# Sixteen of 48 column blocks of a conditioning map, moved from a feed-forward layer to the S5 scans

## The chip, the cores and the metric

One core of one Trainium2 chip runs the whole program in one launch. The metric is the device time of one execution in microseconds, and the lower the better.

## What is computed

The reference is a two-layer trunk for 128 context tokens and 1024 latent tokens of width 1024, in fp32. Every sub-layer is scaled, shifted and gated by a conditioning map of that layer, `w_ada[l]`, which is 1024 × 6144: six vectors of 1024 (shift, scale and gate of the mixer, then of the feed-forward part).

```
for l in range(DEPTH):                                   # DEPTH = 2
    mod = silu(c_in) @ w_ada[l] + b_ada[l]
    sh1, sc1, g1, sh2, sc2, g2 = split(mod, 6)
    h = modulate(rmsnorm(x, norm1_g[l]), sh1, sc1)
    if l % 2 == 0:  m = conv_fourier_mixer(h, ...)       # layer 0
    else:           m, fin = s5_mixer(h, ...)            # layer 1
    x = x + g1 * m
    h = modulate(rmsnorm(x, norm2_g[l]), sh2, sc2)
    x = x + g2 * (silu(h @ w_gate) * (h @ w_up)) @ w_ffn_out[l]
```

`s5_mixer` drives 64 groups of 16 channels through a 64-state complex diagonal recurrence in both directions, then takes GELU and a gated linear unit (GLU).

## The kernel before

**Stages.** Layer 0's mixer, the first feed-forward layer (about 480 to 1300 us), the S5 scans (about 1310 to 1481 us), the GLU, the second feed-forward layer. Big matmuls are three fp32r products each (lines 123 to 125).

**The map of layer 2** (in the code the second of the two layers has the number 1) is made as side work of the first feed-forward layer. The 6144 columns are 48 blocks of 128. For one block, `ada_load` (line 280) brings 512 KB into the tile `araw`, and `ada_rows` (line 299) does eight fp32 matmuls into an `ada` bank (line 304; each is two on the hardware), one copy on ACT into a row tile `arow` (line 306) and a store of the row to `ada1_d` in DRAM. Every few blocks `ada_sums` (line 309) reads the rows back transposed with eight small strided loads (`acol`, line 314), and adds them on POOL into `modt[1]`. `ada_scale` makes the scale vectors from it. The loop at the end of `table_steps` sets the pace: one block at every seventh turn of the tables' side work, the sums of six blocks at a time. All DMAs of this work are issued from ACT's queue. Blocks 32 to 47 are the scale and the gate of the second feed-forward part.

**The scans** run over eight feature tiles f (class `S5`, `run` at line 1243). `front(f)` makes S = E·U on PE (line 1162) and copies it into the pair of tiles D on ACT (line 1168; half of them on VectorE for f = 0). `scan(f)` is twelve operations on VectorE (lines 1184 to 1195) that use the tables T, D and tiles R and V of which there are two each. `back(f)` makes the products Y on PE (M·U at line 1213, fz·state at line 1219), copies them on ACT into y (line 1222), stores y to `yd_d` from ACT's queue (line 1226) and loads it back into `zp`, transposed, from POOL's queue (line 1230). `gelu(f)` on ACT (line 1236) turns zp into a tile of `xall`. `spill(f)` (line 1239) stores a piece of x from POOL's queue. U, E, T, M and fz come in by SP's queue; the scans' input u goes out to `u_d` in DRAM and comes back as U by SP's queue as well. Tiles come from pools with a fixed number of buffers: who asks for a tile whose buffers are all in use waits for the last reader of the oldest.

**The GLU** (`Glu.run`, line 1374) splits the tiles of `xall` into two fp32r halves `zz` on ACT and VectorE (lines 1294, 1295), with the last two `gelu` in between, and starts its products.

The order of the instructions on each engine is laid out by a scheduling layer, not by the text of the code alone.

Of the kernel before, what the change touches and what calls it, by code (L numbers as in the profile page):

```python
# [11 lines left out]
F32 = mybir.dt.float32  # L12
# [8 lines left out]
NF = D // 128  # L21
# [3 lines left out]
CW = 384  # L25
# [31 lines left out]
def kernel(  # L57
# [7 lines left out]
    nc = tc.nc  # L65
    V, S, G, PE = nc.vector, nc.scalar, nc.gpsimd, nc.tensor
    uid = [0]

    def nm(p):
        uid[0] += 1  # L70
        return f"{p}{uid[0]}"
# [24 lines left out]
    ada1_d = dram.tile([128, 48 * 128], F32, name="ada1_d")  # L96
# [199 lines left out]
        PE.matmul(po[:, 0:2], row, sel, start=True, stop=True)  # L296
        V.tensor_scalar(modt[l][:, s, :], po[:, 0:2], vec_a[:, 48 * l + s:48 * l + s + 1], None, op0=OP.add)

    def ada_rows(pool, s, raw):

        ps = aux("ada")
        for k in range(8):
            j = k % 4
            PE.matmul(ps[32 * j:32 * j + 32, :128], cond[:, k, :], raw[:, k, :], start=(k < 4), stop=(k >= 4))  # L304
        row = pool.tile([128, 128], F32, tag="arow", name=nm("arow"), bufs=2)
        S.activation(row, ps[:, :128], AF.Copy)
        nc.scalar.dma_start(ada1_d[:, s * 128:s * 128 + 128], row)

    def ada_sums(pool, b0, nb):

# [523 lines left out]
    def table_steps(P, pool, tb):  # L834
# [156 lines left out]
        raw, ns, summed, turn = ada_load(pool, 1, 0), 0, 0, 0  # L991
        for f in range(8):
            ct = prepare(f, *nxt)
            yield
            for q in range(4):
                if q % 2 == 0:
                    both = []
                if q == 1 and f < 7:
                    nxt = fetch(f + 1)
                for i, _ in enumerate(batch(f, q, ct, both)):  # L1000
                    if ns % 6 == 0 and turn % 7 == 5 and summed < ns:
                        ada_sums(pool, summed, 6)
                        summed = ns
                    if turn % 7 == 0 and ns < 48:
                        ada_rows(pool, ns, raw)
                        ns += 1
                        if ns < 48:
                            raw = ada_load(pool, 1, ns)
                    turn += 1
                    yield  # L1010
# [35 lines left out]
    class S5:  # L1046
# [52 lines left out]
        @staticmethod  # L1099
        def groups(f):  # L1100
            return ((0, 2), (2, 2), (4, 2), (6, 2)) if f in (0, NF - 1) else ((0, 3), (3, 3), (6, 2))

        BUFS = {"U": 4, "T": 2, "T1": 2, "d0": 2, "D": 6, "R": 2, "V": 2, "yz": 3}

# [128 lines left out]
        def gelu(self, f):  # L1233
# [2 lines left out]
            S.activation(zt[:, :LAT].rearrange("p (c t) -> p t c", t=T8), zv[:, :, LX:], AF.Gelu_apprx_tanh)  # L1236
            S.activation(zt[:, LAT:].rearrange("p (c t) -> p t c", t=T8), zv[:, :, :NC_CTX], AF.Gelu_apprx_tanh)

        def spill(self, f):
            cs = slice((NCH - 1) * CW, TOK)  # L1240
            nc.gpsimd.dma_start(x_d[f][:, cs], self.x[f][:, cs])

        def run(self):
            self.front(0)
            for f in range(NF):
                self.scan(f)
                if f + 1 < NF:
                    self.front(f + 1)
                if f + 2 < NF:
                    self.load_e(f + 2)  # L1250
                if f:
                    self.back(f - 1)
                if f + 2 < NF:
                    self.load_in(f + 2)
                if f and f + 1 < NF:
                    self.load_out(f + 1)
                if f + 2 < NF:
                    self.load_t(f + 2)
                    self.decay(f + 2)
                if f > 1:  # L1260
                    with tc.issue_after(self.last.ins):
                        self.gelu(f - 2)
                self.spill(f)
            self.back(NF - 1)

    def states_out(P, fin):
        st = P.t("st")[0:64, :256].rearrange("s (q p r) -> s q p r", q=2, r=2)
        for i in range(2):
            ps = aux("fin")
            PE.transpose(ps[:64, :128], fin[i], ident)  # L1270
            V.tensor_copy(st[:, :, :, i], ps[:64, :128].rearrange("s (q p) -> s q p", q=2))
        nc.sync.dma_start(new_state[0, 0].rearrange("d (k q) p r -> k d q (p r)", q=2),
                          st.rearrange("s q p r -> s q (p r)"))
# [8 lines left out]
    class Glu:  # L1282
# [87 lines left out]
        def run(self, gelu, forms0):  # L1370
            for c in (0, 1):
                for f in range(NF - 2):
                    self.split(f, c)
            for f in (NF - 2, NF - 1):
                with tc.issue_after(self.last.ins):
                    gelu(f)
                for c in (0, 1):
                    self.split(f, c)
            self.weights(0)
            sg = self.products((0, 1), 0)  # L1380
            for f in range(NFK, NF):
                for c in (2, 3):
                    self.split(f, c)
            for c in (0, 1):
                self.load_x(c)
            self.add(sg, 0)
            todo = [(f, c) for f in range(NFK) for c in (2, 3)]
            for i in range(1, NF):
                self.output((0, 1), i)
                for _ in range(2):  # L1390
                    if todo:
                        self.split(*todo.pop(0))
            self.load_x(2)
            self.load_x(3)
            for c in (0, 1):
                self.store_x(c)
            work = None
            for i in range(NF):
                if i == 1:
                    self.norm.finish(0)  # L1400
                    self.norm.finish(1)
                    work = forms0()
                self.output((2, 3), i, work or iter(()))
            for _ in work:
                pass
            for c in (2, 3):
                self.store_x(c)
            for c in (2, 3):
                self.norm.finish(c)
# [342 lines left out]
    with ExitStack() as right:  # L1752
# [4 lines left out]
        with tc.tile_pool(name="act0", bufs=1, reuse_waits="tile") as act, \  # L1757
                tc.tile_pool(name="tmp0", bufs=2, reuse_waits="tile") as tmp0, \
                tc.tile_pool(name="big0", bufs=5, reuse_waits="tile") as big0:
            P = Pools(hp, act, tmp0, 3)  # L1760
# [4 lines left out]
        with tc.tile_pool(name="act1", bufs=1, reuse_waits="tile") as act, \  # L1765
# [5 lines left out]
            def fill():  # L1771
                with tc.tile_pool(name="tb0", bufs=5, reuse_waits="tile") as tb0:
                    yield from tb.build(P, tb0)
                with tc.tile_pool(name="wk", bufs=1, reuse_waits="tile") as wk:
                    g = table_steps(P, wk, tb)
                    yield from g
                    ada_scale(1, 0, G)
                    ada_scale(1, 1, G)

            s5 = {}  # L1780

# [24 lines left out]
        with tc.tile_pool(name="big2", bufs=1, reuse_waits="tile") as big2, \  # L1806
                tc.tile_pool(name="tmp2", bufs=2, reuse_waits="tile") as tmp2:
            P = Pools(None, None, tmp2, 1)
            s5, s5_in = s5["run"], s5["in"]
            s5.begin(P, big2, zq)  # L1810
            for i, _ in enumerate(s5_in.chunk(NCH - 1, s5.load_in)):
                if i == 2:
                    s5.outputs()
            s5.run()
            states_out(P, s5.fin)
    with ExitStack() as right, late as left:
        def pool(name, side, bufs=1):
            st = right if side == "right" else left
# [84 lines left out]
```

## Time and profile before

| | us |
|---|---|
| three executions | 2509.4, 2514.0, 2515.5 |
| median | 2514.0 |
| the profiled execution | 2516.9 |
| its span | 2514.9 |
| PE busy | 2420.1 (96%) |
| DVE busy | 1743.5 (69%) |
| ACT busy | 895.0 (36%) |
| POOL busy | 182.9 (7%) |

The profile is of one execution. A row of a timeline names the start, the time busy, the engine, the line, the operation, output <- inputs, the tile's shape, how often it stands there in a row, and in brackets how long the engine sat idle before it and what released it. "PEclk" is the granted clock of TensorE as a share of its full 2.4 GHz; "DMA share" is the mean busy share of the 16 DMA engines.

### The profile page before, as it was taken

The page shows a single profiled execution, that of the slowest core. Times are in us where ns is not written, and L with a number is a line of the kernel's source. Part 1 is how long each engine was busy: PE and PEld are TensorE (multiplying, and loading weights), DVE is VectorE, ACT ScalarE, POOL GpSimd, SP SyncE. Part 2 cuts the span into 40 slices and gives each one's busy share as a digit, 9 for nine tenths or more (in the row PEclk, how much of TensorE's full clock was granted, in tenths as well). Part 3 has the DMA queues.
Part 4 walks back from the last instruction along what each step waited for, and adds up shares of the span by engine and source line. Part 5 has one row for each costly group of instructions (what it writes and reads, how often), then busy time and mean ns, then how long its engine had stood idle before and what let it go on. Part 6 is the DMA issues. An engine that isn't in the chain of part 4 may idle for free.

```text
span 2514.9 us, 45306 instructions
## 1 busy us (share of the span) xinstructions
PE 2420.1 (96%) x17327; PEld 2344.8 (93%) x17327; DVE 1743.5 (69%) x4619; ACT 895.0 (36%) x1805; POOL 182.9 (7%) x233
## 2 busy tenths in 40 slices
PE   7999999999999999999976899999999999999998
PEld 6999999999999999999976789998999999999998
DVE  7766678988887888887258983658666666645343
ACT  5322443233233333322353552535232232434332
POOL 0000120000000000000020001112000000122110
PEclk9999999999999999999988999999999999999999
DMA  9443342344545455543257973342222212476543
GB/s 261 128 133 94 93 118 62 82 125 120 136 122 134 122 133 132 131 125 82 81 177 261 297 207 106 115 123 85 86 68 70 89 62 88 142 233 206 157 133 103
DMA packets 522680, 328.02 MB, mean 130 GB/s; under 512 B 101000, under 2 KB 492672, under 8 KB 522464
## 3 DMA queue, kind: packets, MB, share of 16 engines
q1 hardware_dynamic: 350432, 236.25, 32.0%
q10 hardware_dynamic: 163680, 58.96, 9.6%
q0 software_dynamic: 8352, 29.92, 3.6%
q8 instruction: 136, 2.23, 0.4%
q14 instruction: 80, 0.66, 0.1%
HBM read 254.04 MB, written 71.01 MB: 129 GB/s over the span
## 4 chain that ended last, share of the span: by engine, by line
PE 81%; DVE 8%; DMA 7%; ACT 2%; issue 1%; ACTq 0%; SPq 0%; POOL 0%; DVEq 0%; POOLq 0%
PE mm L123 19%; PE mm L125 18%; PE mm L124 18%; PE mm L1563 6%; PE mm L1565 6%; PE mm L1564 6%; PE Y L1219 1%; DVE xall L588 1%; DMA yd_d<-y 1%; PE ada L304 1%; DMA zp<-yd_d 1%; DMA hr<-hid_d 1%; DVE tm L831 1%; DMA u_d<-u 1%; PE nst L194 1%
## 5 line engine op out<-in xcount | busy, mean ns | idle before, releaser
L123 PE MATMUL mm<-hh,whi 128*128 128x384 f32 x1392 | 472.5, 339 | 1.1 <-ACT f L448 1.1
L125 PE MATMUL mm<-hh,wlo 128*128 128x384 f32 x1392 | 466.0, 335 | 1.5 <-DVE wlo L117 1.3
L124 PE MATMUL mm<-hl,whi 128*128 128x384 f32 x1392 | 465.8, 335 | 0.0
L117 DVE TENSOR_TENSOR wlo<-wraw,whi 128x1024 fp32r<-128x1024 f32 (+1 forms) x216 | 259.6, 1202 | 227.1 <-ACT whi L116 226.0
L116 ACT ACTIVATE whi<-wraw 128x1024 fp32r<-128x1024 f32 (+1 forms) x218 | 225.7, 1036 | 490.2 <-PE mm L124 363.1
L123 PEld LDWEIGHTS mm<-hh,whi 128*128 128x128 f32 x1392 | 261.5, 188 | 10.9 <-issue 9.0
L125 PEld LDWEIGHTS mm<-hh,wlo 128*128 128x128 f32 x1392 | 261.4, 188 | 4.6 <-issue 2.5
L124 PEld LDWEIGHTS mm<-hl,whi 128*128 128x128 f32 x1392 | 261.6, 188 | 0.2 <-issue 0.2
L588 DVE SCALAR_TENSOR_TENSOR xall<-mm,modt,xall 128x384 f32<-128x384 f32 (+2 forms) x384 | 190.5, 511 | 64.4 <-PE mm L125 63.5
L1563 PE MATMUL mm<-T,wf 128*128 128x288 f32 x640 | 189.6, 296 | 0.0
L1564 PE MATMUL mm<-T,wf 128*128 128x288 f32 x640 | 189.0, 295 | 0.0
L1565 PE MATMUL mm<-T,wf 128*128 128x288 f32 x640 | 188.3, 294 | 0.0
L123 PE MATMUL mm<-hb,whi 128*128 128x384 f32 x528 | 178.6, 338 | 6.9 <-ACT whi L116 6.9
L123 PE MATMUL mm<-hidh,whi 128*128 128x384 f32 x528 | 181.6, 344 | 0.5 <-ACT whi L116 0.5
L125 PE MATMUL mm<-hb,wlo 128*128 128x384 f32 x528 | 178.3, 338 | 1.9 <-DVE wlo L117 1.9
L125 PE MATMUL mm<-hidh,wlo 128*128 128x384 f32 x528 | 177.9, 337 | 0.6 <-DVE wlo L117 0.6
L124 PE MATMUL mm<-hb,whi 128*128 128x384 f32 x528 | 177.7, 337 | 0.0
L124 PE MATMUL mm<-hidl,whi 128*128 128x384 f32 x528 | 177.4, 336 | 0.0
L123 PE MATMUL mm<-zz,whi 128*128 128x288 f32 x512 | 152.4, 298 | 3.1 <-ACT zz L1294 2.1
L124 PE MATMUL mm<-zz,whi 128*128 128x288 f32 x512 | 151.0, 296 | 0.2
L125 PE MATMUL mm<-zz,wlo 128*128 128x288 f32 x512 | 150.9, 296 | 0.0
L185 POOL TENSOR_TENSOR ssq<-ssq,sq 128x384 f32<-128x384 f32 (+1 forms) x75 | 98.4, 1312 | 703.2 <-ACT sq L181 701.0
(388 smaller groups left out, 5454.7 us busy)
## 6 DMA issues: line engine op xcount, KB each, us to landing
wraw<-in_w_ffn_out_dram SPq DMA_DIRECT2D x70, 512.0 KB
wraw<-in_w_ffn_in_dram SPq DMA_DIRECT2D x52, 512.0 KB
araw<-in_w_ada_dram ACTq DMA_DIRECT2D x48, 512.0 KB
wraw<-in_w_glu_dram SPq DMA_DIRECT2D x32, 512.0 KB
araw<-in_w_ada_dram ACTq DMA_DIRECT2D x80, 192.0 KB
wraw<-in_w_out_mix_dram SPq DMA_DIRECT2D x24, 512.0 KB
xall<-in_w_ffn_in_dram SPq DMA_DIRECT2D x20, 512.0 KB
wr<-in_w_ffn_in_dram SPq DMA_DIRECT2D x20, 512.0 KB
```

What stands on the lines that cost most here:

```text
L116: S.activation(hi[:, :n], raw[:, :n], AF.Copy)
L117: eng.tensor_sub(lo[:, :n], raw[:, :n], hi[:, :n].bitcast(F32))
L123: PE.matmul(ps, wh, xs[0], start=start, stop=False)
L124: PE.matmul(ps, wh, xs[1], start=False, stop=False)
L125: PE.matmul(ps, wl, xs[0], start=False, stop=stop)
L185: eng.tensor_add(self.ssq[ch], self.ssq[ch], sq)
L194: PE.matmul(ps[:bw, j:j + 1], part[:, j * bw:(j + 1) * bw], ones, start=part is not sq, stop=part is sq)
L304: PE.matmul(ps[32 * j:32 * j + 32, :128], cond[:, k, :], raw[:, k, :], start=(k < 4), stop=(k >= 4))
L588: V.scalar_tensor_tensor(x[o][:, a:b], ps[:, a - ch * CW:b - ch * CW], gate(l, which, o, s), x[o][:, a:b], op0=OP.mult, op1=OP.add)
L1563: PE.matmul(ps, wh, xh[:, cs], start=kt == 0, stop=False)
L1564: PE.matmul(ps, wh, xl[:, cs], start=False, stop=False)
L1565: PE.matmul(ps, wl, xh[:, cs], start=False, stop=kt == NFK - 1)
```

## The change

The last 16 of the 48 blocks are no longer made in `table_steps` but in a new method `condition(f)` of the scans, two per feature tile, after `spill(f)`. Their loads and the stores of their rows are issued from POOL's queue. `araw` is there a tile with one buffer in the pool `tmp2`; the row is a slice of a tile with the tag "t", three buffers, in the scans' first pool. The pace in `table_steps` goes from a block every 7 turns to one every 11, the sums from 6 blocks to 8. The sums of the 16 blocks and the second scale are made in `Glu.run`, once both x loads are issued, before the first `add`. The final states use a "t" tile of the same pool.

```
-    def ada_rows(pool, s, raw):
+    def ada_rows(row, s, raw, queue):
...
-        row = pool.tile([128, 128], F32, tag="arow", name=nm("arow"), bufs=2)
         S.activation(row, ps[:, :128], AF.Copy)
-        nc.scalar.dma_start(ada1_d[:, s * 128:s * 128 + 128], row)
+        queue.dma_start(ada1_d[:, s * 128:s * 128 + 128], row)
...
-                    if ns % 6 == 0 and turn % 7 == 5 and summed < ns:
-                        ada_sums(pool, summed, 6)
+                    if ns % 8 == 0 and turn % 11 == 8 and summed < ns:
+                        ada_sums(pool, summed, 8)
                         summed = ns
-                    if turn % 7 == 0 and ns < 48:
-                        ada_rows(pool, ns, raw)
+                    if turn % 11 == 0 and ns < S5.ADA:
+                        ada_rows(pool.tile([128, 128], F32, tag="arow", name=nm("arow"), bufs=2), ns, raw, nc.scalar)
                         ns += 1
-                        if ns < 48:
+                        if ns < S5.ADA:
                             raw = ada_load(pool, 1, ns)
...
+        ADA = 32
...
+        def condition(self, f):
+            n = (48 - self.ADA) // NF
+            for s in range(self.ADA + n * f, self.ADA + n * f + n):
+                raw = self.P.tmp.tile([128, 8, 128], F32, tag="araw", name=nm("araw"), bufs=1)
+                nc.gpsimd.dma_start(raw, w_ada[1, :, s * 128:s * 128 + 128].rearrange("(k p) c -> p k c", p=128))
+                row = self.pools[0].tile([128, CW], F32, tag="t", name=nm("arow"), bufs=3)[:, :128]
+                ada_rows(row, s, raw, nc.gpsimd)
...
                 self.spill(f)
+                self.condition(f)
             self.back(NF - 1)
...
             for c in (0, 1):
                 self.load_x(c)
+            ada_sums(self.tmp, S5.ADA, 48 - S5.ADA)
+            ada_scale(1, 1, G)
             self.add(sg, 0)
...
                     ada_scale(1, 0, G)
-                    ada_scale(1, 1, G)
```

How this moves instructions is seen in the order of the built programs. On PE, at the beginning of the scans, behind the last norm (`nrb`), before:

```order
L206 MATMUL nrb_15772<-ident,rq_15740 128x128 x3
L1162 MATMUL S_15844<-U_15781,E_15768 64x145 x4
...
L1162 MATMUL S_15890<-U_15781,E_15770 64x145 x4
L1162 MATMUL S_15930<-U_15790,E_15797 64x145 x6
...
L1162 MATMUL S_15968<-U_15790,E_15799 64x145 x4
L1162 MATMUL S_16016<-U_15982,E_15978 64x145 x6
```

and after:

```order
L206 MATMUL nrb_15498<-ident,rq_15466 128x128 x3
L304 MATMUL ada_15727<-araw_15724,cond 32x128 x8
L304 MATMUL ada_15741<-araw_15738,cond 32x128 x8
L1164 MATMUL S_15570<-U_15507,E_15494 64x145 x4
...
L304 MATMUL ada_15932<-araw_15929,cond 32x128 x5
L1164 MATMUL S_15598<-U_15507,E_15494 64x145 x4
...
L304 MATMUL ada_15932<-araw_15929,cond 32x128 x3
L1164 MATMUL S_15656<-U_15516,E_15523 64x145 x6
...
L304 MATMUL ada_15946<-araw_15943,cond 32x128 x8
L304 MATMUL ada_16138<-araw_16135,cond 32x128 x8
L304 MATMUL ada_16152<-araw_16149,cond 32x128 x8
L304 MATMUL ada_16344<-araw_16341,cond 32x128 x2
L1164 MATMUL S_15770<-U_15708,E_15704 64x145 x6
```

The names with U_15781, U_15790 and U_15982 before (U_15507, U_15516 and U_15708 after) are tiles 0, 1 and 2. Two blocks now stand before S of tile 0, one is split around its second half, and block 3 and those up to the first two matmuls of block 6 stand between S of tile 1 and S of tile 2.

On ACT, where S of tile 1 is copied into its two D tiles, before:

```order
L1168 ACTIVATE D_15928<-S_15962 128x2x145
L1173 ACTIVATE D_15928<-h_15131 128x4
L1168 ACTIVATE D_15929<-S_15938 128x3x145
L1168 ACTIVATE D_15929<-S_15954 128x3x145
L1168 ACTIVATE D_15929<-S_15968 128x2x145
```

and after, where the pair is D_15654 and D_15655:

```order
L1170 ACTIVATE D_15654<-S_15688 128x2x145
L1175 ACTIVATE D_15654<-h_14857 128x4
L305 ACTIVATE arow_15945<-ada_15946 128x128
L1170 ACTIVATE D_15655<-S_15664 128x3x145
L1170 ACTIVATE D_15655<-S_15680 128x3x145
L1170 ACTIVATE D_15655<-S_15694 128x2x145
```

The row of block 3 now stands between the copies of the two tiles. On VectorE those that read tile 1's second D come before the scan of tile 0 (R_15626), here after; before it was the same with other numbers:

```order
L1187 TENSOR_TENSOR V_15753<-T_15529,D_15655 128x1168
L1189 TENSOR_TENSOR D_15655<-T_15527,D_15655 128x1168
L1186 TENSOR_TENSOR R_15626<-T_14851,D_15568 128x584 x2
L1188 TENSOR_TENSOR R_15626<-R_15626,V_15627 128x584
L1190 TENSOR_TENSOR D_15568<-T_14853,D_15568 128x584
```

Nothing moved on VectorE itself. On PE at the end of the scans, where the products Y of tile 6 begin, there were only rows of lines 1213 and 1219 before; after:

```order
L1221 MATMUL Y_16897<-D_16386,fz_16528 128x145
L304 MATMUL ada_16951<-araw_16948,cond 32x128 x8
L1215 MATMUL Y_17005<-U_16523,M_16731 128x145
L1215 MATMUL Y_17006<-U_16523,M_16731 128x145
...
L1221 MATMUL Y_17005<-D_16592,fz_16734 128x145
L304 MATMUL ada_16965<-araw_16962,cond 32x128 x8
```

Between the two blocks stand 15 rows of Y. The same pattern stands at Y of tile 7.

## Rows read from the trace of the kernel before

**Rows 1.** Stretches: us; busy PE, PEld, DVE, ACT, POOL; PEclk, DMA share, GB/s.

```profile
600.00:800.00 200.00, 197.12 (x1439) 188.15 (x1439) 162.66 (x651) 63.53 (x151) 3.83 (x8) 0.99 0.51 129
...
1304.00:1316.00 12.00, 2.15 (x13) 1.69 (x13) 8.19 (x28) 6.60 (x9) 0.54 (x1) 0.59 0.42 123
1316.00:1343.00 27.00, 13.33 (x146) 12.73 (x148) 15.62 (x21) 6.87 (x25) 0.00 (x0) 0.69 1.03 370
...
1402.00:1457.00 55.00, 46.73 (x590) 41.73 (x586) 54.90 (x43) 25.77 (x69) 1.59 (x3) 0.97 0.89 281
1457.00:1481.00 24.00, 23.72 (x298) 20.97 (x294) 22.12 (x33) 8.43 (x14) 1.06 (x2) 1.00 0.66 191
1481.00:1500.00 19.00, 15.96 (x107) 14.48 (x107) 12.49 (x30) 17.88 (x38) 2.33 (x3) 1.00 0.61 183
```

**Rows 2.** Timeline of DVE: tile 1, scan 0, then tiles 4 and 7.

```profile
1331.48 1.38 DVE L1185 TENSOR_TENSOR V<-T,D 128x1168 f32<-128x1168 f32 x1 [4.61 <-ACT D L1173]
1332.89 1.37 DVE L1187 TENSOR_TENSOR D<-T,D 128x1168 f32<-128x1168 f32 x1
1334.86 1.44 DVE L1184 TENSOR_TENSOR R<-T,D 128x584 f32<-128x584 f32 x2 [0.59 <-DMA u_d<-u]
...
1402.87 1.37 DVE L1185 TENSOR_TENSOR V<-T,D 128x1168 f32<-128x1168 f32 x1
...
1457.39 0.77 DVE L1185 TENSOR_TENSOR V<-T,D 128x584 f32<-128x584 f32 x1
```

**Rows 3.** Timeline of PE at the beginning of the scans.

```profile
1317.47 11.21 PE L1162 MATMUL S<-U,E 128*64 128x145 f32 x128 [8.18 <-DMA U<-u_d]
1340.85 5.59 PE L1162 MATMUL S<-U,E 128*64 128x145 f32 x64 [12.16 <-DMA U<-u_d]
```

**Rows 4.** Timeline of PE around one block in the feed-forward layer.

```profile
489.53 0.34 PE L124 MATMUL mm<-hidl,whi 128*128 128x384 f32 x1
489.71 0.34 PE L125 MATMUL mm<-hidh,wlo 128*128 128x384 f32 x1
489.98 0.65 PE L304 MATMUL ada<-araw,cond 128*32 128x128 f32 x16
490.55 0.44 PE L123 MATMUL mm<-hidh,whi 128*128 128x384 f32 x1
490.83 0.34 PE L124 MATMUL mm<-hidl,whi 128*128 128x384 f32 x1
```

**Rows 5.** Line 304: idle time of PE before it (us, times), by releaser.

```profile
  issue: 8.7, 37
```

**Rows 6.** The tile zp: its eight loads (issue in ns), and their landing.

```profile
L1230 POOL DMA_DIRECT2D zp<-yd_d x8: 528/531/539, 1372.6 to 1486.8; - x8
...
DMA to landing us min/median/max: 4.0/5.4/8.2
```

**Rows 7.** The chain that ended last, 1370 to 1500 us: start, us, what.

```profile
1395.20 8.19 DMA zp<-yd_d
1403.47 11.64 DMA yd_d<-y
...
1481.30 4.97 DMA yd_d<-y
1486.82 4.29 DMA zp<-yd_d
```

**Rows 8.** Timeline of POOL: the last store of x before the scans.

```profile
1304.25 0.54 POOL L1241 DMA_DIRECT2D x_d<-xall  x1 [2.76 <-DVE xall L588]
```

**Rows 9.** Timeline of PE: the beginning of Y of tile 6.

```profile
1457.37 0.76 PE L1213 MATMUL Y<-U,M 128*128 128x145 f32 x4
1458.07 0.76 PE L1219 MATMUL Y<-D,fz 64*128 64x145 f32 x8
```

**Rows 10.** Issues of the sums' loads (ns); timeline of ACT at the last gelu.

```profile
L314 ACTq DMA_DIRECT2D acol<-ada_d x64: 366/556/2242, 561.2 to 1146.0; - x64
...
1491.12 2.16 ACT L1236 ACTIVATE xall<-zp 128x1024 f32<-128x1024 f32 x1 [0.96 <-DMA zp<-yd_d]
```

More of the change, by code (lines that the diff above doesn't have):

```diff
@@ L1263, in run, with states_out @@
                 self.spill(f)
+                self.condition(f)
             self.back(NF - 1)
-    def states_out(P, fin):
-        st = P.t("st")[0:64, :256].rearrange("s (q p r) -> s q p r", q=2, r=2)
+    def states_out(pool, fin):
+        st = pool.tile([128, CW], F32, tag="t", name=nm("st"), bufs=3)[0:64, :256].rearrange("s (q p r) -> s q p r", q=2, r=2)
         for i in range(2):
@@ L1814 @@
             s5.run()
-            states_out(P, s5.fin)
+            states_out(s5.pools[0], s5.fin)
     with ExitStack() as right, late as left:
```

## The prediction

> **What bounds the kernel now.** I read the busy times by stretch first, because the change takes work from one stage and puts it into another, and what a microsecond of TensorE is worth differs between the two. From 600 to 800 us, inside the first feed-forward layer, PE is busy 197.1 of 200 us [rows 1]: whatever is taken off PE there comes off the end. In the scan stage (about 1335 to 1457 us) the bound is VectorE: DVE is busy 54.9 of 55 us between 1402 and 1457, PE 46.7 and ACT 25.8 [rows 1]. One feature tile takes (1457.39 − 1402.87) / 3 = 18.17 us of it [rows 2]. So PE has idle time there, but not at its two ends. At the front, 1316 to 1343 us, PE and DVE wait for data: the DMA share is 1.03 at 370 GB/s [rows 1], and PE stood idle 8.18 us before the first S matmuls and 12.16 us before those of tile 2, both times released by U [rows 3]. At the tail, 1457 to 1481, PE is busy 23.72 of 24 us [rows 1]: the Y products of the last two tiles are the critical path.
>
> **The part that is taken out.** Each block is 16 hardware matmuls. At 489.98 us one stands between two ordinary ones: the start before it is 489.71, the start after it 490.55, 0.84 us for what takes 0.18 elsewhere in the same rows (489.53 to 489.71), and the next one starts 0.28 later instead of 0.18 [rows 4]. So a block costs 0.66 + 0.10 = 0.76 us, and 16 cost 12.2. Over all 48 blocks the engine also sat idle 8.7 us under "issue" before them [rows 5], a third of which is 2.9. That bounds the gain by 12.2 and 15.1 us; I take **−14**, nearer the upper end, since the idle time stood in front of these very instructions. The three ways in which the sums are cut differently (blocks of 8, every 11 turns) touch ACT's queue and POOL there, which have time: nothing.
>
> **The front of the scans, the term I am least sure of.** The order of the changed kernel shows what now stands ahead of scan 0. araw has one buffer, so the loads are a chain: load, 16 matmuls, next load. Blocks 0 and 1 stand on PE before S of tile 0, block 2 is split around its second half, and block 3 comes after S of tile 1. On ACT the copy of block 3's row stands ahead of the three copies that make tile 1's second D. And on DVE V and D of tile 1 stand ahead of R of tile 0, that is, ahead of the whole of scan 0. So scan 0 now waits for the fourth load of a serial chain. Its price is four landings. The trace shows no such load at this place. The nearest rows are the zp loads, the same queue and 580 KB instead of 512: 4.0, 5.4 and 8.2 us to landing (least, median, most) [rows 6], 8.19 us in the one of the critical chain where the DMA was full, while the y store of 580 KB took 11.64 [rows 7]. I take about 5.7 for the first two, at 1304 to 1316 where the share is 0.42 [rows 1], and 8.2 for the other two, where it is 1.03. The last spill is issued at 1304.25 and takes 0.54 [rows 8], so block 0 lands at 1310.5; its matmuls cost 0.65 at full clock [rows 4] and about 1.15 here by estimate, since the granted clock of this stretch is 0.59 [rows 1]: 1311.7. Block 1: 1317.5, done 1318.6. Only then S of tile 0 begins, 1.1 us later than the 1317.47 of before [rows 3]. Block 2 lands at 1326.8; the second half of S(0), 2.8 us (11.21 us for 128 matmuls [rows 3], so 2.8 for 32), stands between its first five matmuls and its last three, so it is done, and block 3's load issued, at about 1330.5. Block 3 lands at 1338.7 and is done at 1339.8. Then the row's copy, three copies of some 0.45 (1.6 us together by estimate), V 1.38 and D 1.37 [rows 2]: R of tile 0 starts at about 1344.2 instead of 1334.86 [rows 2], which is **+9**. With landings of 4.0 the chain ends at about 1331, right behind S of tile 1, and nearly all of it is hidden in the 8 and 12 us that PE waited anyway: +1. With 11.6 for the last two it is +17. Three more blocks stand before S of tile 2; by the same landings it ends near 1363, Y of tile 0 near 1375, and scan 2, which needs the R and V buffers that Y of tile 0 frees, would begin at about 1376: just enough, so they add nothing. The loads of U and E that share the queue engines are delayed at most by the added bytes, 4 × 512 KB at 370 GB/s = 5.7 us, a second way to the same few microseconds.
>
> **The middle.** From tile 2 on one or two blocks of 0.65 us [rows 4] fall to each 18.17 us, of which PE has 18.17 − 18.17 × 46.73/55 = 2.7 idle [rows 1]. They hide, but for the last four. Two blocks stand around S of tile 6 and two around S of tile 7, and the Y product of tile 5 ends at 1457.37, when scan 7's first V starts at 1457.39 (it needs the buffer) [rows 2, 9]: no slack at all. Four times 0.65 is 2.6, plus a wait for the second load of a pair: **+3**, between 0 and 6.
>
> **The tail.** The last four blocks stand before and inside Y of tiles 6 and 7, when nothing but PE works toward the end: 4 × 0.6 = 2.4 us for certain. In each pair the second load can start only when the first block's matmuls are done, and only 15 hardware rows of Y (about 2.2 us by estimate: 12 rows of M and fz take 1458.07 − 1457.37 + 0.77 = 1.47 [rows 9]) separate the two. With a landing of 5.4 [rows 6] PE waits 5.4 + 0.1 − 2.2 = 3.3 us twice. Together **+9**, between 6.2 (4.0 us) and 14.6 (8.2 us). What follows the last Y (the store of y, 4.97, its load, 4.29, gelu on ACT) [rows 7] is moved as it is.
>
> **The start of the GLU.** The sums of the 16 blocks are eight small strided loads, issued from ACT's queue. In before such an issue took 0.366, 0.556 and 2.242 us (least, median, most) [rows 10]. Seven stand ahead of the last splits, 7 × 0.56 = 3.9 us, on an engine busy 17.88 of 19 us [rows 1] that waited only 0.96 before the last gelu [rows 10]. Some of it falls beside work that PE already has: **+2**, between 0 and 4. POOL's adds and the scale behind them are needed only in the next norm: nothing.
>
> **Sum.** −14 + 9 + 3 + 9 + 2 = +9. The profiled execution took 2516.9 us, 2.9 above the median of 2514.0, so 2525.9 on its footing is **2523** as a median. 0.3% is 7.5 us, about what a measurement of this kernel can tell from no change; +9 lies just beyond.
>
> **The rivals.**
> *Quick loads.* If a 512 KB load lands in 4.5 to 5 us even in the full stretch, the chain of four ends at about 1332, its delay shrinks to +3 (R at 1332 + 1.6 + 2.75 = 1336.3, and 1.5 for the added bytes), the tail to +7, the middle to +1 and the GLU's start to +1: −14 + 12 = −2, 2512. For it: the median landing of zp is 5.4 with 580 KB [rows 6]. Against it: the one zp that met a full DMA took 8.19 and the store beside it 11.64 [rows 7].
> The Trainium skill's page "DMA: Bandwidth & Descriptors", section "Queues, rings and completion order", says that each DMA engine takes turns between the queues that have work, a packet from each. By that rule a load on POOL's queue gets half of the engines beside SP's queue however long that one is, some 5 us by estimate for 512 KB at half of 370 GB/s with its start, which is this rival's time of 2512. The trace disagrees in the 8.19 us.
> *Everything hides.* With landings of 4.0 us throughout, the whole gain of up to 15.1 remains, less the tail's 6.2, which no landing removes, and 1 at the front: −8, 2506. This needs the least row of the trace everywhere.
> *The transfers become the bound.* 16 × 512 KB = 8.4 MB are added to stretches with a share of 0.89 to 1.03 at 281 to 370 GB/s [rows 1], 23 to 30 us of all engines. The ring of y store (11.64), zp load (8.19) [rows 7] and gelu, one per tile, takes 19.8 us of them against a tile's 18.17 [rows 2]; if each of the six middle tiles is stretched by some 1.5 us of added transfer, that is +9 on top: +18, 2532. It decides once a tile's two loads lengthen the ring by more than its slack. In before the share falls to 0.66 only after 1457 [rows 1].
> *A blocked descriptor writer.* DVE is busy without a gap in the scans, and POOL's loads would have to wait for it. Here the zp issues took 0.53 us while DVE was busy 54.9 of 55 us [rows 6, 1], so nothing is added for it.
> The Trainium skill's page "SBUF — State Buffer", section "A bandwidth-pool intuition that's wrong (but worth ruling out)", gives such a DMA 3.1 us instead of 0.62 beside a DVE copy; 16 of them at 2.5 us more would be 40 us by estimate if all were on the path. The zp rows speak against it.
>
> **How the numbers follow.** My forecast (+9, its own range +3 to +17) has 0.47. Quick loads 0.28, everything hidden 0.12, the transfers 0.11, the blocked writer 0.02. Range: 2508 to 2538, which leaves out the lowest part of the hidden case and the largest sums. Of the forecast all but a little lies above +7.5 or close below it; I count that little with the quick loads: faster by over 0.3% 0.12, within 0.3% 0.30, slower 0.58.
>
> **What would show it.** In the changed profile: the feed-forward layer some 14 us shorter; the first three S groups waiting for araw instead of U; R of tile 0 at about 1330 in its own time (1344 less 14); Y of tile 6 interrupted for some 3 us by a wait for araw; landings of araw between 5 and 9 us. It would be wrong if araw lands in 4 us beside a full DMA, if S of tile 0 starts as early as before, or if the scans' tiles take more than 18.2 us each.

## The result and the profile after

The changed kernel takes 2569.5 us (median of 4), the kernel before on the same chip 2514.6: a ratio of 1.0214, 95% interval 1.0200 to 1.0227, 55 us slower. Slower was forecast, but by 9 us, and 2569.5 lies far outside 2508 to 2538. The profiled execution has a span of 2565.9 us, 51.0 above the 2514.9 of before.

The same stretches as in [rows 1], from the changed kernel (us; busy PE, PEld, DVE, ACT, POOL; granted clock, DMA share, GB/s):

```profile
600.00:800.00 200.00, 195.60 (x1375) 187.66 (x1376) 162.91 (x655) 62.83 (x146) 0.70 (x3) 1.00 0.45 114
800.00:1000.00 200.00, 193.51 (x1360) 184.89 (x1359) 168.39 (x683) 59.63 (x135) 1.87 (x8) 1.00 0.46 112
...
1402.00:1457.00 55.00, 47.58 (x590) 42.19 (x588) 49.45 (x39) 23.45 (x64) 6.49 (x10) 0.91 1.01 338
1457.00:1481.00 24.00, 18.55 (x230) 15.74 (x228) 17.64 (x14) 8.54 (x23) 3.46 (x5) 0.86 0.59 182
1481.00:1500.00 19.00, 12.31 (x128) 10.39 (x126) 18.63 (x24) 3.88 (x8) 3.43 (x5) 0.73 0.68 209
```

The kernel before has for 800 to 1000 us, a row that [rows 1] leaves out:

```profile
800.00:1000.00 200.00, 198.03 (x1446) 187.52 (x1444) 169.94 (x684) 61.26 (x140) 3.08 (x9) 1.00 0.52 127
```

Two things stand there. In the feed-forward layer PE is *less* busy in the same time, 195.6 and 193.5 of 200 us against 197.1 and 198.0 (197.8 and 195.0 in a second profile of the kernel before): the matmuls are gone and idle time has come instead. In the scans VectorE is no longer full (49.45 of 55), PE is idle too, and the granted clock has fallen to 0.73 at the end.

To see where the 51 us arise I read the start of the same instruction in both profiles. Each step is the difference of two neighbouring marks:

| stage, up to | before | after | added here |
|---|---|---|---|
| last norm ahead of the scans (nrb) | 1308.4 | 1306.4 | −2.0 |
| scan 0 begins (R of tile 0) | 1334.9 | 1344.4 | +11.5 |
| scan 2 begins (V of tile 2) | 1366.5 | 1378.2 | +2.2 |
| scan 6 begins (V of tile 6) | 1439.2 | 1456.4 | +5.5 |
| scan 7 begins (V of tile 7) | 1457.4 | 1481.3 | +6.7 |
| last Y done (fin on PE) | 1480.3 | 1525.6 | +21.4 |
| GLU's first product | 1481.7 | 1527.5 | +0.6 |
| second feed-forward layer, first product of T and wf (its weight load) | 1733.7 | 1783.3 | +3.7 |
| end of the span | 2514.9 | 2565.9 | +1.4 |

So the feed-forward layer gave 2 us instead of 14, and the scans took 47. The waits behind it, timeline of VectorE after (against [rows 2]):

```profile
1341.70 1.37 DVE L1187 TENSOR_TENSOR V<-T,D 128x1168 f32<-128x1168 f32 x1 [10.44 <-ACT D L1175]
1344.40 1.44 DVE L1186 TENSOR_TENSOR R<-T,D 128x584 f32<-128x584 f32 x2
...
1378.22 1.38 DVE L1187 TENSOR_TENSOR V<-T,D 128x1168 f32<-128x1168 f32 x1 [2.11 <-PE Y L1221]
...
1456.44 1.38 DVE L1187 TENSOR_TENSOR V<-T,D 128x1168 f32<-128x1168 f32 x1 [5.45 <-DMA T<-t_d]
...
1481.34 1.45 DVE L1187 TENSOR_TENSOR V<-T,D 128x584 f32<-128x584 f32 x2 [6.66 <-PE Y L1221]
```

And on PE, where the blocks' loads had not landed (the groups of line 304, after):

```profile
1307.87 1.08 PE L304 MATMUL ada<-araw,cond 128*32 128x128 f32 x16 [0.60 <-DMA araw<-in_w_ada_dram]
1316.39 1.08 PE L304 MATMUL ada<-araw,cond 128*32 128x128 f32 x16 [7.44 <-DMA araw<-in_w_ada_dram]
...
1338.85 1.08 PE L304 MATMUL ada<-araw,cond 128*32 128x128 f32 x16 [5.50 <-DMA araw<-in_w_ada_dram]
...
1441.47 1.08 PE L304 MATMUL ada<-araw,cond 128*32 128x128 f32 x16 [5.06 <-DMA araw<-in_w_ada_dram]
...
1466.85 1.08 PE L304 MATMUL ada<-araw,cond 128*32 128x128 f32 x16 [5.45 <-DMA araw<-in_w_ada_dram]
...
1492.10 1.08 PE L304 MATMUL ada<-araw,cond 128*32 128x128 f32 x16 [6.69 <-DMA araw<-in_w_ada_dram]
...
1512.63 1.08 PE L304 MATMUL ada<-araw,cond 128*32 128x128 f32 x16 [4.27 <-DMA araw<-in_w_ada_dram]
```

The last four are the second blocks of the pairs at S of tiles 6 and 7 and inside Y of tiles 6 and 7. In the group of line 304 between 1300 and 1530 us PE stood idle 56.7 us for araw (busy, mean ns, idle before):

```profile
L304 PE MATMUL ada<-araw,cond 128*32 128x128 f32 x256 | 15.5, 362 | 56.7 <-DMA araw<-in_w_ada_dram 56.7
```

Each of these waits has a tail of its own. Around the one at 1492 us, PE's rows that [rows 9] shows at 0.76 take 1.33 and 1.34; the granted clock is 0.51 from 1492 to 1499 and 1.00 from 1499 on:

```profile
1493.11 1.33 PE L1221 MATMUL Y<-D,fz 64*128 64x145 f32 x6
1494.37 1.33 PE L1215 MATMUL Y<-U,M 128*128 128x145 f32 x4
1495.63 1.34 PE L1221 MATMUL Y<-D,fz 64*128 64x145 f32 x8
...
1499.37 0.76 PE L1215 MATMUL Y<-U,M 128*128 128x145 f32 x4
```

And the same by stretch (columns as above):

```profile
1492.00:1499.00 7.00, 6.90 (x54) 5.92 (x56) 6.97 (x10) 0.28 (x1) 1.44 (x2) 0.51 0.52 169
1499.00:1505.00 6.00, 6.00 (x80) 5.37 (x76) 2.59 (x5) 0.82 (x2) 0.00 (x0) 1.00 0.02 4
```

That is 6.3 us of Y (1493.11 to 1499.37) for what takes about 3.3 at full clock: a wait of 6.69 us costs some 9.6. Behind the waits of 5.06, 5.45 and 4.27 us the granted clock was 0.50 for 6.0, 4.3 and 6.6 us, which lost 2 to 3 us each.

### The profile page after: what moved, and what is told of

Its sections match the earlier page's. It is cut to its first block, busy times and chain, and to the rows that moved or that the text cites. A ratio compares the mean times of both kernels' runs of the same rounds, so it can differ in the third digit from the quotient of the medians.

```text
span 2565.9 us, 45279 instructions
## 1 busy us (share of the span) xinstructions
PE 2435.5 (95%) x17327; PEld 2355.8 (92%) x17327; DVE 1740.5 (68%) x4619; ACT 896.2 (35%) x1805; POOL 202.3 (8%) x256
```

## Experiments

Chips differ by some us (the kernel before: 2514.6, 2519.9, 2520.5, 2521.7 and 2515.8 us as the median beside each group of runs), so ratios are against the kernel before on the same chip, and stages are compared by the time *between* marks: last norm to last Y (172 us before), and GLU's first product to the first one of T and wf in the second feed-forward layer (252 us before; called the GLU's time below). Each profile is of one execution. In the profiles without blocks in the scans, the kernel before and the relieved ones further down among them, last norm to last Y spreads from 171.9 to 176.1 us, so a few us there tell nothing.

**The feed-forward part alone.** In `run`, the new call is taken out, and the sums read rows 16 to 31 in place of 32 to 47:

```
-                self.condition(f)
...
-            ada_sums(self.tmp, S5.ADA, 48 - S5.ADA)
+            ada_sums(self.tmp, S5.ADA, 48 - S5.ADA, S5.ADA - 16)
```

> The 16 blocks are left out altogether (32 are made in the feed-forward layer, the sums at the GLU's start read other rows). My theory: the feed-forward layer gives back only what the profile after shows, the last norm 2.0 us earlier than before, because VectorE's table work is next in line there; the scans are as before; the GLU starts 5 us later for the sums' loads on ACT. So about 2517, within 0.3% of before. Rival: the 14 us are really saved and something in the scans takes them back; then 2514 - 14 + 5 = 2505.

Measured 1.0043 (1.0025 to 1.0062), 11 us slower than before, though 16 blocks less are made. Neither expectation held. The GLU took 255.8 us instead of 252, as in the changed kernel, but the feed-forward layer gave nothing that the profile shows: the last norm stands at 1313.7 us. (The profiled execution, 2524.0 us, was the fastest of the five.)

**The same with the sums' loads on SP's queue** (`queue.dma_start` with `nc.sync` in `ada_sums`).

> As the run without the 16 blocks, but the eight loads of the sums are issued from SP's queue. Theory: the issues on ACT stood between the last splits and cost 5 us there, so this is 4 to 5 us faster than the run without the blocks, about 2512. Rival: the GLU's start is late for the scans' tail alone; then no difference between the two.

Measured 1.0042 (1.0026 to 1.0058): no difference to the run before, but not for the rival's reason. The sums are dear wherever they are issued. SP takes 14.78 us to issue the eight loads. POOL's adds of the sums, which here stand ahead of POOL's x loads (in the run before, behind the first two), begin only at 1500.61, and the x loads follow at 1502.17. VectorE's first add to x waits 8.62 us for them, the low halves of the weights (`wlo`) stand behind that add, and PE waits 8.21 us for `wlo`; the GLU takes 261.7 us. The timeline of SP, POOL, VectorE and PE:

```profile
1482.58 14.78 SPq L315 DMA_DIRECT2D acol<-ada_d  x8
1510.36 1.50 SPq L113 DMA_DIRECT2D wraw<-in_w_glu_dram  x2
...
1500.61 0.32 POOL L316 TENSOR_TENSOR acol<-acol 128x64 f32<-128x64 f32 x1 [12.09 <-ACT whi L116]
...
1502.17 1.87 POOL L1311 DMA_DIRECT2D xall<-x_d  x2
...
1508.73 0.46 DVE L1352 TENSOR_TENSOR xall<-xall,sg 128x288 f32<-128x288 f32 x1 [8.62 <-DMA xall<-x_d]
1509.11 2.35 DVE L117 TENSOR_TENSOR wlo<-wraw,whi 128x1024 fp32r<-128x1024 f32 x2
...
1510.38 0.61 PE L125 MATMUL mm<-zz,wlo 128*128 128x288 f32 x1 [8.21 <-DVE wlo L117]
```

The next weights on SP's queue are not what PE waits for: SP was done with the eight loads at 1497.36 and issued the weights at 1510.36, when `wlo` freed their buffer. That POOL's adds waited for the landing of the eight loads is my reading; the profile names another releaser, which ended at about that time. The theory was right that the issues stood in ACT's way, and missed that POOL's x loads would stand behind the sums.

**The kernel before again**, and **blocks and sums left out**: in `Glu.run` the sums are replaced by a fill of zeros.

```
-                self.condition(f)
...
-            ada_sums(self.tmp, S5.ADA, 48 - S5.ADA)
+            G.memset(modt[1][:, S5.ADA:48], 0.0)
```

> The kernel before, unchanged, profiled on the chip of the next three, so that stages can be compared on one chip. From the last norm ahead of the scans to the end it should repeat the first profile within 1 us; if the last norm stands some us from 1308.4, that is how far one profile of the feed-forward layer can be trusted.

> The 16 blocks and their sums are left out altogether: what taking them out of the feed-forward layer is worth by itself. Theory (VectorE's table work is next in line there): between 0 and -4 us against before, PE waiting 10 us for e at line 920 and 4 to 6 for wlo. Rival (PE alone bounds the layer): -12 to -15.

Measured: the last norm of the kernel before stands at 1313.5 us here, 5 us later than in its first profile, so one profile of that layer is good to 5 us only; from there to the last Y both profiles agree (171.9 and 172.3 us). Without blocks and sums: 1.0013 (1.0001 to 1.0025), so 16 blocks less on PE are worth nothing, or less. On this chip the last norm is at 1313.1 against 1313.5; the 3 us that are lost stand behind it, between last norm and last Y (175.3 us), within the spread named above. Over all ten profiles here with 32 blocks and VectorE's work as before (the changed kernel's two among them), from the first `et` of the tables to the last norm it is 812.7 us in the mean (809.0 to 817.9), over the two of the kernel before 812.9.

The stretch from 480 to 1180 us of the kernel before, then of the kernel without blocks and sums, and what PE waited for between 480 and 1295 us (us in total, times, longest), in the same order; `e` is a tile of the tables that PE transposes into `et`, `wlo` the low half of a weight tile:

```profile
480.00:1180.00 700.00, 691.33 (x4996) 658.18 (x4995) 587.27 (x2348) 215.93 (x497) 9.67 (x28) 1.00 0.51 125
```

```profile
PE et L921 <- DVE e L832: 3.1, 5, 1.1
PE mm L125 <- DVE wlo L117: 3.1, 2, 2.4
```

```profile
480.00:1180.00 700.00, 681.04 (x4743) 652.59 (x4743) 585.01 (x2352) 212.39 (x481) 3.66 (x14) 1.00 0.44 111
```

```profile
PE et L920 <- DVE e L831: 11.0, 9, 3.2
PE mm L125 <- DVE wlo L117: 8.1, 7, 2.3
```

PE does 10.3 us less in the same 700, and stands idle for VectorE instead: 13 us more in two kinds of waits, in place of 2.2 us ahead of the blocks.

**Less work on VectorE, with and without the 16 blocks.** In `batch`, for the second e:

```
-            cmul(e[1], pe[0], B[1], pe[1], B[0], tmp, OP.add)
+            V.tensor_mul(e[1], pe[0], B[1])
```

> As the run without blocks and sums, and of the second e in each of the 32 table batches one product and one sum on VectorE are left out as well, 32 x (0.612 + 0.422) = 33 us of its work. Theory: with VectorE relieved the blocks' price comes out, some 10 to 14 us less than the run without blocks and sums. Rival (the waits have another cause, the order or the pace of the blocks): no change against it.

> The kernel before with the same 33 us of VectorE's work left out. Theory: PE was busy 99% there, so little can come of it, 0 to -4 us; the difference to the run with 16 blocks less and the same relief is then the blocks' true price on PE, 10 to 14 us. Rival: VectorE bounded the layer already before; then -10 or more.

Measured 0.9972 (0.9961 to 0.9983) without the blocks and 0.9987 (0.9977 to 0.9997) with all 48. So relieving VectorE brings 10 us when the blocks are gone (1.0013 to 0.9972) and 3 us when they are there. That shows that VectorE's table work is what the layer waits for once the blocks are out, and it refutes the rival named for the first of the two (the order or the pace of the blocks alone). A run with fewer blocks at the old pace was not made. The blocks' own price comes out at 0.15%, 4 us, not the 10 to 14 expected, and the traces show why: the relief was smaller than 33 us (between 480 and 1180 us VectorE's busy time fell by 18.5 and 23.5 us against the runs with its full work), and without the blocks PE still waits 8.3 us for e, in four waits, which it does not do with them. What PE waited for between 480 and 1295 us, first without the blocks, then with all 48, both relieved:

```profile
PE et L920 <- DVE e L904: 8.3, 4, 2.8
PE mm L125 <- DVE wlo L117: 1.7, 3, 0.8
```

```profile
PE ada L304 <- ACT ko L966: 3.7, 2, 2.8
PE mm L125 <- DVE wlo L117: 3.2, 3, 1.9
```

Of the 10 us, 7 stand ahead of the last norm in the profiles (1313.1 to 1306.4 us), and of the 3 us all (1313.5 to 1310.4).

**One load for all blocks.** `araw` is loaded once, at tile 0, and all 16 products use it:

```
+                if s == self.ADA:
+                    self.raw = self.P.tmp.tile([128, 8, 128], F32, tag="araw", ...)
+                    nc.gpsimd.dma_start(self.raw, ...)
+                raw = self.raw
```

> Only the first block is loaded, all 16 products use it (15 blocks come out wrong). All matmuls, row copies and stores stay, the chain of loads is gone; the matmuls then stand together ahead of the scan of tile 2. Theory (the loads' chain is the price): the matmuls fit into the 8 and 12 us that PE waits for U, the scans are as before, so -2 + 5 for the GLU and up to 4 for the rows' copies and stores: 2517 to 2521. Rival (the matmuls and rows themselves): 16 x 1.1 us of half clock ahead of the scans plus the copies on ACT, 2530 or more.

Measured 1.0063 (1.0044 to 1.0081), 16 us slower, 5 more than the feed-forward part alone. Last norm to last Y takes 177.5 us: with the loads' chain gone, some 42 of the 47 us are gone. But the program then has all products ahead of scan 2, so this alone doesn't tell the chain from the places. The total lies at the edge of the rival's range, but only 6 of the 16 us are the scans'; 5 are the GLU's.

**The loads alone**, two at tile 0, then two behind each tile's zp load, products left out:

```
+                    with tc.issue_after(self.zload.ins):
+                        self.condition(f)
```

> The 16 loads alone, two at the beginning and two behind each tile's zp load on POOL's queue; products, rows and stores left out. Theory (PE's waits are the price, not the traffic): the same 8.4 MB then cost little, up to the 5.5 us that a T load was late in the profile after: 2515 to 2524. Rival (traffic): the added 24 us of full transfer in stretches with a share near 1 slow the scans; most of the 55 us stays, 2540 or more.

Measured 1.0074 (1.0057 to 1.0091), 19 us slower. Last norm to last Y takes 176.5 us, 4.6 above before and 0.4 above the most of the runs without loads, so the same 8.4 MB by themselves don't slow the scans by much. The GLU takes 262.2 us, because the last loads on POOL's queue stand ahead of what it needs: the zp load of the last tile is issued at 1504.58, behind the last load of a block, which had waited 7.56 us for the one before it to land, and PE waits 8.3 us in the GLU for `zz` (2.1 before).

**The blocks on tiles 0 to 5 only**, one buffer as before:

```
-            n = (48 - self.ADA) // NF
-            for s in range(self.ADA + n * f, self.ADA + n * f + n):
+            at = (32, 34, 37, 40, 43, 46, 48, 48, 48)
+            for s in range(at[f], at[f + 1]):
```

> The changed kernel with the 16 blocks on tiles 0 to 5 (2, 3, 3, 3, 3, 2) and none on tiles 6 and 7; still one buffer, so the same chain of loads. Theory (every wait of PE for a load inside the Y products, and the half clock behind it, is paid in full once nothing but PE works): the tail's 21 us go, the front's 11 and the middle's waits stay; 25 to 38 us above before. Rival (the added work and traffic cost the same wherever they stand): no change, 50 to 55 above.

Measured 1.0256 (1.0242 to 1.0270), 65 us slower: worse than the change, and above both expectations. Here my reading fell that a wait in the tail is paid in full and one beside the scans is not. The tail is as before (V of tile 7 to last Y 23.7 us), but now each tile waits; timeline of VectorE:

```profile
1430.05 1.38 DVE L1187 TENSOR_TENSOR V<-T,D 128x1168 f32<-128x1168 f32 x1 [9.74 <-PE Y L1221]
...
1461.82 1.38 DVE L1187 TENSOR_TENSOR V<-T,D 128x1168 f32<-128x1168 f32 x1 [13.53 <-PE Y L1221]
...
1489.19 1.37 DVE L1187 TENSOR_TENSOR V<-T,D 128x1168 f32<-128x1168 f32 x1 [9.14 <-PE Y L1221]
```

Scan f waits for the R and V buffers that Y of tile f−2 reads. A wait of PE inside S or Y thus stops VectorE as soon as it is longer than PE's spare time in a tile, in the middle as at the end.

**Three buffers, loads a tile ahead.** The two buffers of the late zp tiles serve as well, each group of up to three is loaded (`load_blocks`) behind a tile's zp load and multiplied (`make_blocks`) one tile later behind that tile's Y; the sums' loads go out on POOL's queue behind the x loads:

```
+                    with tc.issue_after(self.zload.ins), tc.issue_after(self.lasty.ins), tc.issue_after(self.last.ins):
+                        self.make_blocks()
+                        self.load_blocks(f)
```

> The same 16 blocks in three buffers (the two of the late zp tiles serve until tile 6), each group loaded behind a tile's zp load and multiplied one tile later behind that tile's Y, copied behind its y; the sums' loads go out on POOL's queue behind the x loads. Theory (the price of the change is PE and ACT standing in order behind loads that have not landed): nothing waits now, what stays is the work on ACT, the traffic and 2 blocks in the tail, 2 to 8 us above before. Rival (traffic and matmuls as such): 20 or more above.

Measured 1.0111 (1.0096 to 1.0125), 28 us slower: 27 us better than the change, but not the 2 to 8 expected. Scan 0 begins as in the kernel before (27.1 us after the last norm, 26.4 and 26.9 before), so the front's 11.5 are gone. But three loads at once beside full transfers take 5.1 to 13.3 us to land, 9.4 in the median; PE still waited 20.1 us for them, and one scan 11.54 us for its table T, which SP had issued only at 1429.24, behind E, whose buffer a late S held:

```profile
1418.15 1.08 PE L304 MATMUL ada<-araw,cond 128*32 128x128 f32 x16 [7.66 <-DMA araw<-in_w_ada_dram]
...
1428.33 0.82 SPq L1118 DMA_DIRECT2D E<-e_d  x2
1429.24 0.94 SPq L1126 DMA_DIRECT2D T<-t_d  x2
...
1439.38 1.38 DVE L1187 TENSOR_TENSOR V<-T,D 128x1168 f32<-128x1168 f32 x1 [11.54 <-DMA T<-t_d]
```

The GLU took 263.2 us, the most of all, with the sums on POOL's queue. The weight load that SP issued at 1527.01, among the eight loads of the sums, was there only for ACT's row at 1544.11. Row of ACT, and the stretch (columns as above):

```profile
1544.11 1.06 ACT L116 ACTIVATE whi<-wraw 128x1024 fp32r<-128x1024 f32 x1 [12.26 <-DMA wraw<-in_w_glu_dram]
```

```profile
1532.00:1536.00 4.00, 4.00 (x33) 4.00 (x32) 0.34 (x1) 0.00 (x0) 1.88 (x2) 1.00 1.15 59
```

The DMA engines are full there, with 59 GB/s moved.

**An eighth of each load**, and **the changed kernel again** on the same chip. Only one slice of eight is loaded, and used eight times:

```
-                nc.gpsimd.dma_start(raw, w_ada[1, :, ...].rearrange("(k p) c -> p k c", p=128))
+                nc.gpsimd.dma_start(raw[:, 0:1], w_ada[1, 0:128, ...].rearrange("(k p) c -> p k c", p=128))
+                raw = raw[:, 0:1, :].to_broadcast([128, 8, 128])
```

> The changed kernel with loads of 64 KB instead of 512 (one of the eight slices, used eight times, so 16 blocks come out wrong). The one buffer, the chain of loads and the places of the products on PE, ACT and POOL are the same, save that one block more stands ahead of scan 2's S. Theory (the time that a load takes to land beside full transfers is the price): a load lands in 3 to 4 us, the front falls from 11 us to 1 to 3, the four inner waits of tiles 6 and 7 from 4 to 7 us each to 1 to 3, without the half clock behind them, and the T load is on time; 12 to 22 above before. Rival (places and chain as such, whatever the bytes): 40 or more above.

> The changed kernel unchanged, on the same chip as the one with small loads, so that the two can be compared stage by stage: 50 to 58 above before again, and the same waits ahead of the last blocks.

Measured 1.0119 (1.0095 to 1.0143) and 1.0198 (1.0177 to 1.0219): 27 and 48 us as medians. Neither forecast for the small loads was right: they take away 29 of the 47 us that the scans lose, and leave 18. The changed kernel repeats itself to 1 us or two in every stage, though its 48 us are a little under the 50 to 58 expected. Landing of araw (least, median, most), and line 304 on PE between 1300 and 1530 us, first with the small loads, then the changed kernel again:

```profile
DMA to landing us min/median/max: 2.0/4.2/6.5
```

```profile
L304 PE MATMUL ada<-araw,cond 128*32 128x128 f32 x256 | 14.2, 346 | 32.6 <-DMA araw<-in_w_ada_dram 27.9 <-ACT arow L305 4.6
```

```profile
DMA to landing us min/median/max: 4.6/7.5/9.4
```

```profile
L304 PE MATMUL ada<-araw,cond 128*32 128x128 f32 x256 | 15.8, 368 | 58.5 <-DMA araw<-in_w_ada_dram 58.5
```

So some 60% of the scans' loss goes with the 448 KB more of each load, and 40% stays with the chain as such: issue, landing of even 64 KB, product, next issue. The smaller loads also take traffic from the others; what traffic alone costs, the loads alone have shown (at most 4.6 us). How full the DMA engines were between issue and landing goes with the landing: in the changed kernel the three loads with a DMA share of 0.44 to 0.46 landed in 4.6 us, the twelve with 0.79 or more in 6.0 to 9.3; the small ones took 2.0 to 2.2 us at up to 0.46, and 2.6 to 6.5 at 0.86 or more.

**Products on POOL.** To relieve VectorE for good, one product of each complex multiplication into e is made on POOL (`G.tensor_mul(tmp, ...)` in `batch`), in the kernel before and with the placed blocks:

> The kernel before with one of the two products of each complex multiplication into e made on POOL, 64 x 0.61 = 39 us off VectorE. With 33 us left out it gained 3 us, so 0 to -4 us if POOL is in time; slower if VectorE now waits for POOL.

> Both together: the placed blocks and the products on POOL. Theory: with VectorE relieved, taking 16 blocks out of the feed-forward layer pays 7 to 10 us, as in the run that left 33 us of VectorE's work out; 0 to -6 us against before, 7 to 10 below the placed blocks alone. Rival (products on POOL come too late for e): no better than the placed blocks alone.

Measured 1.0025 (1.0014 to 1.0037) and 1.0089 (1.0076 to 1.0102). In the kernel before it loses 6 us: PE waits 5.2 us for e (3.1 before on another chip), and VectorE is busy 581 us of the 700 instead of 587, so the 39 us were not taken off it in effect. VectorE's rows show where they went. The sum into the first e, while POOL makes its second product, takes 702 ns in the mean instead of 418, up to 999, and VectorE stands idle 15.9 us in front of it for POOL's first product; the sum into the second e, with POOL done, takes 418:

```profile
L905 DVE TENSOR_TENSOR e<-e,tm 128x256 f32<-128x256 f32 x32 | 22.5, 702 | 15.9 <-POOL tm L903 15.9
L910 DVE TENSOR_TENSOR e<-e,tm 128x256 f32<-128x256 f32 x32 | 13.4, 418 | 0.9
```

With the blocks placed it gains 5 to 7 us against them, so the first part of that expectation holds in kind, but PE still waits 10.2 us for e, and the kernel stays 22 us above before. No version here that does all the work beats the kernel before.

## Why the prediction was wrong, step by step

**What bounds the kernel** was half right. PE's 197.1 of 200 us said that nothing else could be later *by much*; it did not say how much. VectorE, at 163 to 170 of 200 us there, entered no term, as if it had room. It makes e and wlo in order, in bursts, and was ready just in time; with 12 us less on PE it is late.

**The part taken out, −14: this step failed.** The 0.76 us per block were about right as PE's own work: 10.3 us less busy in 700. But an item that is taken off a 99% busy engine is worth that only up to the next engine's slack, and the sum had no line for it. Measured up to the last norm: −2.0 in the profile, 0 in the mean of ten, −0.4 without blocks and sums on one chip; in the waits, PE's 13 us more for VectorE's e and `wlo`. The further 2.9 us were misread: the 8.7 us of [rows 5] are idle time of PE's weight loads; PE's matmuls themselves stood idle 2.9 us ahead of line 304 in all, twice, for ACT.

**The front, +9: right in kind and nearly in size.** Scan 0 does wait for the fourth serial load, and starts at 1344.40 where 1344.2 was worked out. The landings assumed, 5.7 twice and 8.2 twice, were 4.9, 7.0, 6.6 and 9.3. Since the stage now started 2 us earlier, it cost 11.5. (Of its bounds, the upper one is 16 by its own terms, 9.3 and twice 3.4, not 17.) Blocks 4 to 6 then added 2.2 that I had put at nothing: Y of tile 0 ended 2.11 us after scan 2 could have begun.

**The middle, +3: mis-sized, 12.2 measured.** That Y of tile 5 has no slack was nearly right (scan 7 overwrites V, which Y of tile 5 had read by about 1456.5, 0.9 us ahead), and the wait for the second load of a pair was named, but given under 1 us. It is 5.06 and 5.45 us, and 2 to 3 us each are lost at half clock behind it. The first of them also delays Y of tile 4, and with it V of tile 6, where the timeline names T; with the changed kernel run again a wait of 5.02 us at the same place is put down to Y.

**The tail, +9: mis-sized, 21.4 measured.** The sum had the four blocks and two waits of 3.3. The waits are 6.69 and 4.27 us (9.0 and 6.6 us from a load's issue to its product, where the sum had a landing of 5.4). The rest, 21.4 − 11.0 − 2.4 = 8 us, is mostly the half clock behind them: 6 us in the rows of Y and 1 in the two blocks, for which the sum had nothing here, although [rows 1] shows the clock at 0.59 and 0.69 where PE waits. The 15 rows of Y between two blocks were also misread as 15 on the hardware: they are 30, and took 2.7 us, not 2.2.

**The GLU's start, +2: 4.3 measured.** Issues of up to 2.56 us stand among the last splits; it came out a little beyond the bounds (0 to 4).

By size, then, the sum missed by 12 us in the part taken out (a term that forgot VectorE), by 12 in the tail and by 9 in the middle (terms that had the landings too short and no half clock), and by 5 in the front and 2 in the GLU.

**Of the rivals,** quick loads and everything hidden are refuted by the landings. For the blocked descriptor writer nothing speaks: POOL's issues of araw take 0.89 to 0.91 us beside a busy VectorE. The transfers as the bound are refuted as a cause by themselves (loads alone: +4.6 in the scans), and yet a load lands slowly where the transfers are full (4.6 us at a DMA share of 0.46, 6.0 to 9.3 above 0.79): the slow landing and a place where all of PE stands behind it had to come together. The loads landed in 6.8 us in the median, up to 9.3. By the turns between queues that the Trainium skill's page "DMA: Bandwidth & Descriptors", section "Queues, rings and completion order", describes, I had estimated some 5; the trace doesn't agree with that estimate.

What stays open: how much the blocks would be worth with VectorE relieved in full (PE still waited 8.3 us for it), and where all of the 6 us go that products on POOL cost the kernel before; its profile, 2521.4 us, was one of the fastest of 12 and shows no loss of that size.

## What to carry to other kernels

Before work is taken off a full engine, look for the second engine's slack in that stage, and enter it in the sum; the 12 us of matmuls that hid a nearly late VectorE cost nothing here. Work put beside a loop that another engine bounds is free, by these runs, only if its data have landed when its turn in the order comes: one buffer makes every load a wait of the whole engine, and what the engine's outputs release (here R and V, two tiles later) turns that into a wait of the bound. A wait of 4 to 7 us on PE cost 2 to 3 more here at half clock behind it.

## What the runs showed of the hardware

- Behind each of the last four waits, 4.3 to 6.7 us long, PE's granted clock was 0.50 or 0.51 (1.2 GHz) for the next 4 to 7 us and back near 1.00 after that; in 1481 to 1500 us it was 0.73 in the mean, 1.00 before the change [rows 1].
- A load of 64 KB took 4.2 us to land in the median, one of 512 KB 6.8 to 7.5, in the same places of the scans: eight times the bytes, not twice the time. Either lands sooner where the DMA engines are half idle (2.0 to 2.2 and 4.6 us at a share of 0.46 or less).
- Eight loads of the sums move little, but where they ran beside a weight load the DMA engines were full (a share of 1.15 at 59 GB/s). They held up the GLU by 4 us from ACT's queue and by 10 from SP's, where 14.78 us pass until all are issued; with the placed blocks and the sums on POOL's queue it took 11 us longer.
- A sum of 128x256 on VectorE took 0.42 us alone and up to 1.0 while POOL multiplied tiles of the same size.
